# Padding the halves of an activation tile, a rotation's product in place, and two weight splits moved forward, in a two-layer decoder trunk

## The chip, the cores and the metric

The kernel runs on one core of a Trainium2 chip. Its time is the device time of one execution in microseconds (us), and the median of several executions counts. One execution was taken by the hardware profiler; the page and the answers of its trace that are quoted below come from that one. The engines are PE (TensorE, matmul), PEld (TensorE's loading of weights), DVE (VectorE), ACT (ScalarE), POOL (GpSimd) and SP (SyncE, which here only issues DMAs).

## The reference

A trunk of two layers on 256 tokens of width 2048, all in float32. Layer 0 mixes tokens by multi-scale retention with 8 heads (query and key 256 wide, value 512), layer 1 by a gated short convolution; each is followed by a SwiGLU of width 5632. Each sub-layer is normed, scaled and shifted by vectors that come from the conditioning vector c, and its output is gated and added to x.

```python
c_act = jax.nn.silu(c)
for i in range(DEPTH):
    mod = (c_act @ w_mod[i] + b_mod[i])[:, None, :]
    sh1, sc1, g1, sh2, sc2, g2 = jnp.split(mod, 6, axis=-1)
    h = (rms_norm(x, norm1_g[i]) * (1.0 + sc1) + sh1).astype(x.dtype)
...
        y = retention_mixer(h, cos, sin, ret_w_in[j], ret_w_out[j])
...
    x = (x + g1 * y).astype(x.dtype)
    h = (rms_norm(x, norm2_g[i]) * (1.0 + sc2) + sh2).astype(x.dtype)
    x = (x + g2 * swiglu(h, ffn_w_in[i], ffn_w_out[i])).astype(x.dtype)
return rms_norm(x, final_g).astype(x.dtype)
```

In the retention, q and k are rotated: `[t1 * cos - t2 * sin, t2 * cos + t1 * sin]` for the two halves t1, t2 of a head.

## The kernel before

**Layout.** The width lies on the partitions: x is 16 tiles of 128 by 256 tokens. The weights were put on the host into one array, `w_all`, in the order of their use, in chunks of 128 by 2048 floats.

**Precision.** A float32 factor is used as two parts of the type float32r: hi, the value rounded, and lo, what is left. A product is hi x hi + hi x lo + lo x hi. So an activation tile holds two halves of 256 columns, its hi in front of its lo. For h these halves lie in one tile, `h_all` (16 tiles x 2 halves x 258 columns; the 2 columns behind each half take the shift, so that a norm can be applied after the product). The other activation tiles, `mid` (input of the second matmul of the SwiGLU and of the convolution) and `rm` (the same for the retention), hold 2 x 256 columns end to end.

**Weights.** `fetch` (L293) loads a chunk into one of 3 buffers `raw`. `prepare` makes one half of a chunk, called a part, ready: ACT casts it to `hi` (L312), DVE subtracts to get `lo` (L315). There are 4 buffers of `hi` and of `lo`. `take` hands the weights to PE in 128 columns at a time and calls `prepare` when a part is used up, so that up to three parts are in hand.

**Matmuls.** `product` (L357, L360) does a block of 128 output rows with two matmuls: the weights' hi past both halves of the activation at once, 512 columns, and their lo past the first half, 256 columns. These two are called a pair. `packed` (L397 to L399) uses three matmuls of 256 columns, and puts two blocks into one PSUM bank. For the values, `by_token` (L372 to L374) takes slices of h as the stationary tile and streams 512 columns of weights. `normed` (L516 to L518) does the first columns of a sub-layer with 258 columns, before the norm is known.

**The start.** The first stretch of about 190 us interleaves the norm and modulation of layer 0 (its rows of h are made one at a time: sums of `w_mod` with c by DVE, L642; scale and shift by ACT, L667 and L670; lo by DVE, L671) with four spans of the retention's input product, `RET_SPANS`. A span runs over some of the 16 rows for some heads, holds 4 to 8 banks of sums, and at its end the sums are put aside by `held`: copied by ACT (L629), or added by DVE to what lies there (L626). Heads 0 to 3 are finished later; head 4 is done whole in the last span, and its sums stay in PSUM (`ahead`). In the start the order of ACT and DVE is the order in which the code is written (`manual_schedule`); PE's order is so throughout. Elsewhere a scheduler orders ACT, DVE, POOL and SP. The loads of a stage are all issued by SP, which waits for the buffer of one load before it issues the next.

**The rotation.** `rope` (L806 to L814) multiplies the sums of q or k by cos into `qa` (512 columns), by sin into `qb` (two operations of 256 columns that exchange the halves), then subtracts and adds halves, and splits the result into hi and lo. Its input is a tile `qs` where earlier sums were added (heads 0 to 3), PSUM otherwise.

Of the kernel before, what the change touches and what calls it, by code (L numbers as in the profile page):

```python
# [11 lines left out]
F32R = mybir.dt.float32r  # L12
I32 = mybir.dt.int32
AF = mybir.ActivationFunctionType
ALU = mybir.AluOpType
PSUM = bass.MemoryType.PSUM

P = 128
D = 2048
S = 256  # L20
KT = D // P
# [27 lines left out]
STEPS = (8, 8, 20)  # L49
RAW_BUFS = 3  # L50
PART_BUFS = 4

Q0, K0, V0, G0 = 0, HEADS * DK, 2 * HEADS * DK, 2 * HEADS * DK + HEADS * DV
SH1, SC1, GT1, SH2, SC2, GT2 = range(6)
# [71 lines left out]
RET_SPANS, RET_HEADS = ret_in_groups()  # L126
# [61 lines left out]
def trunk(ctx: ExitStack, tc: tile.TileContext, x_in, c_in, pos_in, w_mod, cols_in, tab_in, w_all, out):  # L188
    nc = tc.nc
    const = ctx.enter_context(tc.tile_pool(name="const", bufs=1))  # L190
    work = ctx.enter_context(tc.tile_pool(name="work", bufs=2))
    wpool = ctx.enter_context(tc.tile_pool(name="wpool", bufs=PART_BUFS))
    ps = ctx.enter_context(tc.tile_pool(name="ps", bufs=8, space=PSUM))
# [3 lines left out]
    def name(s):  # L197
        serial[0] += 1
        return f"{s}_{serial[0]}"

    def tmp(tag, shape=(P, S), dtype=F32, pool=work, bufs=None):
        return pool.tile(list(shape), dtype, tag=tag, name=name(tag), bufs=bufs)
# [78 lines left out]
    def needed(layer, which, last=KT - 1):  # L281
        while any(m[:2] == (layer, which) and m[2] <= last for m in todo):
            modulation(*todo.pop())
# [7 lines left out]
    def fetch():  # L291
        raw = wpool.tile([P, CHUNK], F32, tag="raw", name=name("raw"), bufs=RAW_BUFS)
        nc.sync.dma_start(raw, w_all[n_fetched[0]])  # L293
        n_fetched[0] += 1
        fetched.append(raw)

    def prepare(between=None):
        n = prepared[0]
        if n == n_halves:
            return  # L300
        prepared[0] += 1
        i = n * HALF % CHUNK
        if i == 0:
            if not fetched:
                fetch()
            raws[:] = [fetched.pop(0)]
            while first <= units[0] < early and len(fetched) < RAW_BUFS - 1 and n_fetched[0] < w_all.shape[0]:
                fetch()
        raw = raws[0][:, i : i + HALF]
        hi = wpool.tile([P, HALF], F32R, tag="hi", name=name("hi"))  # L310
        lo = wpool.tile([P, HALF], F32R, tag="lo", name=name("lo"))
        nc.scalar.copy(hi, raw)  # L312
        if between:
            between()
        nc.vector.tensor_tensor(lo, raw, hi.bitcast(F32), op=ALU.subtract)  # L315
        ready.append((hi, lo))
# [18 lines left out]
    def bank():  # L335
        return ps.tile([P, 2, S], F32, tag="bank", name=name("bank"))
# [139 lines left out]
    def modulated(h, j, rb, layer, norm):  # L476
        shifted(h, scaled(j, rb, layer, norm), j, layer, norm)

    hpool = ctx.enter_context(tc.tile_pool(name="hpool", bufs=1))

    h_all = hpool.tile([P, KT, 2, S + 2], F32R, tag="h", name="h")
    h = [h_all[:, j, :, :S] for j in range(KT)]

    def scaled_only(layer, norm, j):
# [8 lines left out]
    def normed(accs, layer, norm, g):  # L493

        needed(layer, SH2 if norm else SH1)
        shift = mod_s[layer][norm].unsqueeze(2).to_broadcast([P, KT, 2])  # L500
        ends = [h_all[:, :, i, S:] for i in range(2)]
        nc.scalar.copy(ends[0], shift)
        nc.vector.tensor_tensor(ends[1], shift, ends[0].bitcast(F32), op=ALU.subtract)
        banks = [bank().rearrange("p a b -> p (a b)")[:, : S + 2] for _ in g.cols]
        made = [0]

        def more(n):
            while made[0] < n:
                modulated(h[made[0]], made[0], root, layer, norm)
                made[0] += 1  # L510

        for k in g.ks:
            rows = [h_all[:, k, i, :] for i in range(2)]
            for c, pt in zip(g.cols, banks):
                hi, lo = take(g, k, c)
                nc.tensor.matmul(pt, hi, rows[0], start=k == 0, stop=False)  # L516
                nc.tensor.matmul(pt, hi, rows[1], start=False, stop=False)  # L517
                nc.tensor.matmul(pt, lo, rows[0], start=False, stop=k == KT - 1)  # L518
            if k == ROOTS_AT:
                r = norm_roots(norm_sums(accs), D)  # L520
            elif k == SPREAD_AT:
                root = tmp("rb", bufs=1)
                nc.scalar.copy(root, norm_spread(r))
            elif k > SPREAD_AT:
                more(min(k, made[0] + 2))
        more(KT)
        paced(len(g.cols) * len(g.ks))

        def total(pt, dst=None):
            end = tmp("end", (P, 1), bufs=2)  # L530
            nc.scalar.copy(end, pt[:, S : S + 1])
            t = tmp("low", bufs=3)
            nc.vector.tensor_tensor(t, pt[:, :S], root, op=ALU.mult)
            dst = tmp("sum", bufs=4) if dst is None else dst
            nc.scalar.activation(dst, t, AF.Identity, bias=end)
            return dst

        return [lambda dst=None, pt=pt: total(pt, dst) for pt in banks]
# [27 lines left out]
    with ExitStack() as inner:  # L566
# [46 lines left out]
        sin = rm.tile([P, S], F32, tag="sin", name="sin")  # L613
        cos = rm.tile([P, S], F32, tag="cos", name="cos")
        ahead = {}
# [15 lines left out]
        with tc.tile_pool(name="start", bufs=1) as sp:  # L631
# [59 lines left out]
            with tc.manual_schedule(engines={mybir.EngineType.DVE, mybir.EngineType.Activation}):  # L691
# [16 lines left out]
                for i in range(0, D, 2 * S):  # L708
                    pt = bank().rearrange("p a b -> p (a b)")
# [24 lines left out]
                pt = norm_sums([acc[0][:, 0, :]])  # L734
# [23 lines left out]
                pts = packed(RET_SPANS[0], h, before=before, between=both_reduced, banks=banks)  # L758
# [20 lines left out]
            def span(g):  # L779
                n = g.n // 2  # L780
                return packed(
                    g, h, before=lambda k: more(n), between=lambda k: more(n), banks=[bank() for _ in range(n)]
                )

            with tc.manual_schedule(engines={mybir.EngineType.DVE, mybir.EngineType.Activation}):
                for i, pt in enumerate(span(RET_SPANS[1])):
                    held((2 + i // 4, i % 4), pt)
                pts = span(RET_SPANS[2])
                for i, pt in enumerate(pts):
                    if i < 4:  # L790
                        held(divmod(i, 4), pt)
                    else:
                        due.append((step[0] + 0.2 * (i - 4), lambda i=i, pt=pt: held(divmod(i, 4), pt)))
                due.sort(key=lambda d: d[0])
                for i, pt in enumerate(span(RET_SPANS[3])):
                    ahead[4, i] = pt
                while due:
                    due.pop(0)[1]()
# [2 lines left out]

        rp = inner.enter_context(tc.tile_pool(name="rpool", bufs=1))

        def rope(s, tag):
            a = tmp("qa", (P, 2, S), pool=rp, bufs=1)
            nc.vector.tensor_tensor(a, s, cos.unsqueeze(1).to_broadcast([P, 2, S]), op=ALU.mult)  # L806
            b = tmp("qb", (P, 2, S), pool=rp, bufs=1)
            nc.vector.tensor_tensor(b[:, 0, :], s[:, 1, :], sin, op=ALU.mult)
            nc.vector.tensor_tensor(b[:, 1, :], s[:, 0, :], sin, op=ALU.mult)
            nc.vector.tensor_tensor(a[:, 0, :], a[:, 0, :], b[:, 0, :], op=ALU.subtract)  # L810
            nc.vector.tensor_tensor(a[:, 1, :], a[:, 1, :], b[:, 1, :], op=ALU.add)
            dst = rp.tile([P, 2, 2, S], F32R, tag=tag, name=name(tag))
            nc.scalar.copy(dst[:, 0, :, :], a)
            nc.vector.tensor_tensor(dst[:, 1, :, :], a, dst[:, 0, :, :].bitcast(F32), op=ALU.subtract)  # L814
            return dst
# [83 lines left out]
        def pair(head, i):  # L899

            g = RET_HEADS[head][0][i]
            if not g.ks:
                return [ahead[head, n] for n in ((i,) if i < 2 else (2, 3))]
            sums = packed(g, h)
            for j, pt in enumerate(sums):
                key = (head, i + j)
                if key in tag_of:
                    free.append(tag_of.pop(key))
                if key in ahead:
                    s = tmp("qs", (P, 2, S), pool=rp, bufs=1)  # L910
                    nc.vector.tensor_tensor(s, ahead[key], pt, op=ALU.add)
                    sums[j] = s
            return sums

        def projections(head):
            q = rope(*pair(head, 0), "q")
            k = rope(*pair(head, 1), "k")
            v = values(head, RET_HEADS[head][1])
            sp = scores(head, q, k)
            sg = [gate(s) for s in pair(head, 2)]  # L920
            asides.extend(mixed(head, sp, v, sg))
            since[0] = 0
# [48 lines left out]
    for i, g in enumerate(CONV_IN):  # L971
        pending += [sums(g)] if i else normed(acc, 1, 0, g)
        while len(pending) >= 3:
# [3 lines left out]
            b, c, u = pb(tmp("bsum", pool=mpool, bufs=2)), pc(), pu()  # L977
# [73 lines left out]
```

## Time and profile before

| what | value |
|---|---|
| median of 3 runs | 2645.53 us (2645.07 to 2647.69) |
| the profiled execution | 2641.89 us |
| its span, first to last instruction | 2640.1 us |
| granted TensorE clock | 0.998 of full speed |
| loaded from HBM | 682.99 MB, 259 GB/s over the span |

How to read the rows below. In rows of groups: the line of the code, engine, operation, what is written and what it is made from, its shape, how often; then the busy time in us, the mean length of one in ns; then the engine's idle time just before, and what ended it. Busy time is the time in which at least one instruction of the group ran. PE's matmuls overlap: the next one begins before the last one's results are all written. In rows of a time line: start in us, length in us, engine, line, operation, tiles, how many were merged; in brackets the idle time before the first and what ended it. In rows of waits: who waited <- for whom, total us, how often, the longest.

### The profile page before, as it was taken

The page shows a single profiled execution, that of the slowest core. Times are in us where ns is not written, and L with a number is a line of the kernel's source. Part 1 is how long each engine was busy: PE and PEld are TensorE (multiplying, and loading weights), DVE is VectorE, ACT ScalarE, POOL GpSimd, SP SyncE. Part 2 cuts the span into 40 slices and gives each one's busy share as a digit, 9 for nine tenths or more (in the row PEclk, how much of TensorE's full clock was granted, in tenths as well). Part 3 has the DMA queues.
Part 4 walks back from the last instruction along what each step waited for, and adds up shares of the span by engine and source line. Part 5 has one row for each costly group of instructions (what it writes and reads, how often), then busy time and mean ns, then how long its engine had stood idle before and what let it go on. Part 6 is the DMA issues. An engine that isn't in the chain of part 4 may idle for free.

```text
span 2640.1 us, 38225 instructions
## 1 busy us (share of the span) xinstructions
PE 2608.1 (99%) x15220; PEld 2291.2 (87%) x15220; DVE 1990.3 (75%) x2543; ACT 1244.8 (47%) x1770; POOL 146.6 (6%) x230
## 2 busy tenths in 40 slices
PE   7999999999999999999999999999999999999998
PEld 5888889888889888888888898888988888888887
DVE  7998878777698877777777888888886765555554
ACT  5644443444455444344444454444554443444443
POOL 0000001010000011110100001100000000000000
PEclk9999999999999999999999999999999999999999
DMA  9976668776686877777777768777677655555553
GB/s 397 391 273 256 258 242 317 258 271 259 251 300 243 314 283 272 273 283 283 287 270 282 268 224 321 280 281 262 253 277 263 248 219 191 190 191 187 183 190 127
DMA packets 96950, 687.58 MB, mean 260 GB/s; under 512 B 10753, under 2 KB 12545, under 8 KB 13825
## 3 DMA queue, kind: packets, MB, share of 16 engines
q1 hardware_dynamic: 96770, 685.13, 70.0%
q8 instruction: 119, 1.95, 0.3%
q14 instruction: 61, 0.50, 0.1%
HBM read 682.99 MB, written 2.10 MB: 259 GB/s over the span
## 4 chain that ended last, share of the span: by engine, by line
PE 76%; issue 19%; DVE 2%; DMA 1%; ACT 1%; POOL 0%; DVEq 0%; POOLq 0%; ACTq 0%
PE bank L357 35%; PE bank L360 18%; PE bank L372 4%; PE bank L373 4%; PE bank L374 4%; PE bank L399 2%; PE bank L398 2%; PE bank L397 2%; PE bank L517 1%; PE bank L516 1%; PE bank L518 1%; DVE raw L642 1%; DMA raw<-w_all 1%; PE bank L869 1%; DVE lo L315 1%
## 5 line engine op out<-in xcount | busy, mean ns | idle before, releaser
L315 DVE TENSOR_TENSOR lo<-raw,hi 128x1024 fp32r<-128x1024 f32 x912 | 1111.5, 1222 | 551.6 <-ACT hi L312 549.3
L312 ACT CAST hi<-raw 128x1024 fp32r<-128x1024 f32 x912 | 953.2, 1050 | 1088.9 <-PE bank L357 649.0
L357 PE MATMUL bank<-h,hi 128*128 128x512 f32 x3296 | 1155.2, 395 | 0.0
L360 PE MATMUL bank<-h,lo 128*128 128x256 f32 x3296 | 924.4, 280 | 0.0
L357 PEld LDWEIGHTS bank<-h,hi 128*128 128x128 f32 x3296 | 622.6, 189 | 145.3
L360 PEld LDWEIGHTS bank<-h,lo 128*128 128x128 f32 x3296 | 622.0, 189 | 0.0
L357 PE MATMUL bank<-mid,hi 128*128 128x512 f32 x1604 | 556.3, 393 | 0.0
L360 PE MATMUL bank<-mid,lo 128*128 128x256 f32 x1604 | 444.9, 277 | 0.6 <-DVE lo L315 0.6
L246 DVE SCALAR_TENSOR_TENSOR raw<-raw,cb 128x2048 f32<-128x2048 f32 x160 | 365.4, 2284 | 11.7 <-DMA raw<-w_mod 11.3
L357 PEld LDWEIGHTS bank<-mid,hi 128*128 128x128 f32 x1604 | 300.7, 187 | 69.4
L360 PEld LDWEIGHTS bank<-mid,lo 128*128 128x128 f32 x1604 | 301.3, 188 | 0.9 <-DVE lo L315 0.9
L372 PE MATMUL bank<-hi,h 128*128 128x512 f32 x512 | 202.7, 396 | 0.0
L373 PE MATMUL bank<-lo,h 128*128 128x512 f32 x512 | 201.9, 394 | 0.0
L374 PE MATMUL bank<-hi,h 128*128 128x512 f32 x512 | 201.9, 394 | 0.0
L357 PE MATMUL bank<-rm,hi 128*128 128x512 f32 x496 | 174.2, 396 | 0.0
L399 PE MATMUL bank<-h,lo 128*128 128x256 f32 x512 | 145.6, 284 | 9.1 <-DVE lo L315 9.1
L397 PE MATMUL bank<-h,hi 128*128 128x256 f32 x512 | 144.9, 283 | 2.5 <-ACT h L670 2.5
L398 PE MATMUL bank<-h,hi 128*128 128x256 f32 x512 | 144.8, 283 | 0.5 <-DVE h L671 0.5
L360 PE MATMUL bank<-rm,lo 128*128 128x256 f32 x496 | 138.5, 279 | 0.0
L374 PEld LDWEIGHTS bank<-hi,h 128*128 128x128 f32 x512 | 96.3, 188 | 22.7
L372 PEld LDWEIGHTS bank<-hi,h 128*128 128x128 f32 x512 | 96.6, 189 | 19.6
L373 PEld LDWEIGHTS bank<-lo,h 128*128 128x128 f32 x512 | 96.4, 188 | 19.6
(152 smaller groups left out, 2239.3 us busy)
## 6 DMA issues: line engine op xcount, KB each, us to landing
raw<-w_all SPq DMA_DIRECT2D x456, 1024.0 KB, 4.8
raw<-w_mod SPq DMA_DIRECT2D x192, 1024.0 KB, 5.0
x<-x_in SPq DMA_DIRECT2D x4, 512.0 KB, 5.7
out<-out SPq DMA_DIRECT2D x5, 256.0 KB, 3.4
decay<-tab_in SPq DMA_DIRECT2D x8, 128.0 KB, 2.2
out<-out SPq DMA_DIRECT2D x3, 128.0 KB, 2.5
out<-out SPq DMA_DIRECT2D x1, 384.0 KB, 2.7
cols<-cols_in SPq DMA_DIRECT2D x1, 160.0 KB, 8.8
```

The lines of the kernel that those rows point to most:

```text
L246: nc.vector.scalar_tensor_tensor(raw, raw, 1.0, cb, op0=ALU.mult, op1=ALU.mult, accum_out=total)
L312: nc.scalar.copy(hi, raw)
L315: nc.vector.tensor_tensor(lo, raw, hi.bitcast(F32), op=ALU.subtract)
L357: nc.tensor.matmul(pt, hi, h, start=fresh and k == g.ks[0], stop=False, skip_group_check=True)
L360: nc.tensor.matmul(pt[:, 1, :], lo, h[:, 0, :], start=False, stop=last and k == g.ks[-1], skip_group_check=True)
L372: nc.tensor.matmul(o, ht[:, 0, :], hi, start=first, stop=False)
L373: nc.tensor.matmul(o, ht[:, 0, :], lo, start=False, stop=False)
L374: nc.tensor.matmul(o, ht[:, 1, :], hi, start=False, stop=last)
L397: nc.tensor.matmul(pt, hi, h[:, 0, :], start=first, stop=False, skip_group_check=True)
L398: nc.tensor.matmul(pt, hi, h[:, 1, :], start=False, stop=False, skip_group_check=True)
L399: nc.tensor.matmul(pt, lo, h[:, 0, :], start=False, stop=last, skip_group_check=True)
L516: nc.tensor.matmul(pt, hi, rows[0], start=k == 0, stop=False)
```

## The change

Three edits. The halves of h lie 272 columns apart (1088 bytes) where they lay 258 apart (1032 bytes). The rotation multiplies both halves by sin in one operation of 512 columns, which writes over its input where that input is the kernel's own (`ours`: sums that were held or put into `ahead`), and into a tile `qs` otherwise; subtraction and addition read the exchanged halves; the tile `qb` is gone. At the ends of the second and third span `prepare` is called once in front of `held`, so the cast and subtraction of one more part stand in front of the copies or additions on ACT and DVE, and with them the load that `prepare` issues on SP.

```diff
+PAD = 16
...
-    h_all = hpool.tile([P, KT, 2, S + 2], F32R, tag="h", name="h")
+    h_all = hpool.tile([P, KT, 2, S + PAD], F32R, tag="h", name="h")
...
-        ends = [h_all[:, :, i, S:] for i in range(2)]
+        ends = [h_all[:, :, i, S : S + 2] for i in range(2)]
...
-            rows = [h_all[:, k, i, :] for i in range(2)]
+            rows = [h_all[:, k, i, : S + 2] for i in range(2)]
...
-                for i, pt in enumerate(span(RET_SPANS[1])):
+                pts = span(RET_SPANS[1])
+                prepare()
+                for i, pt in enumerate(pts):
                     held((2 + i // 4, i % 4), pt)
                 pts = span(RET_SPANS[2])
+                prepare()
                 for i, pt in enumerate(pts):
...
-        def rope(s, tag):
+        def rope(s, tag, ours):
...
-            b = tmp("qb", (P, 2, S), pool=rp, bufs=1)
-            nc.vector.tensor_tensor(b[:, 0, :], s[:, 1, :], sin, op=ALU.mult)
-            nc.vector.tensor_tensor(b[:, 1, :], s[:, 0, :], sin, op=ALU.mult)
-            nc.vector.tensor_tensor(a[:, 0, :], a[:, 0, :], b[:, 0, :], op=ALU.subtract)
-            nc.vector.tensor_tensor(a[:, 1, :], a[:, 1, :], b[:, 1, :], op=ALU.add)
+            b = s if ours else tmp("qs", (P, 2, S), pool=rp, bufs=1)
+            nc.vector.tensor_tensor(b, s, sin.unsqueeze(1).to_broadcast([P, 2, S]), op=ALU.mult)
+            nc.vector.tensor_tensor(a[:, 0, :], a[:, 0, :], b[:, 1, :], op=ALU.subtract)
+            nc.vector.tensor_tensor(a[:, 1, :], a[:, 1, :], b[:, 0, :], op=ALU.add)
...
-            q = rope(*pair(head, 0), "q")
-            k = rope(*pair(head, 1), "k")
+            q = rope(*pair(head, 0), "q", (head, 0) in ahead)
+            k = rope(*pair(head, 1), "k", (head, 1) in ahead)
```

## Prediction

> **What bounds the kernel now.** I read the page's table of engines first, then its costliest groups, then the waits of PE, and then groups and time lines of single stretches.
>
> ```profile
> span 2640.1 us, 38225 instructions
> PE 2608.1 (99%) x15220; PEld 2291.2 (87%) x15220; DVE 1990.3 (75%) x2543; ACT 1244.8 (47%) x1770; POOL 146.6 (6%) x230
> ```
>
> The span lies in an execution of 2641.89 us, 1.8 us more. The runs' median, 2645.53, is 3.6 us above that execution, and I add these 3.6 us to every sum. PE is busy 99%; what isn't busy stands in the waits of PE:
>
> ```profile
> PE bank L399 <- DVE lo L315: 9.1, 6, 2.3
> PE bank L433 <- DVE sq L733: 3.2, 1, 3.2
> PE bank L397 <- ACT h L670: 2.5, 1, 2.5
> PE bank L360 <- DVE lo L315: 0.6, 1, 0.6
> ...
> 260.00:400.00 140.00, 140.00 (x753) 119.86 (x752) 112.88 (x153) 63.56 (x88) 8.60 (x13) 1.00 0.67 247
> 400.00:600.00 200.00, 200.00 (x1159) 175.45 (x1158) 159.93 (x196) 86.43 (x111) 21.99 (x37) 1.00 0.78 285
> ```
>
> (The last two are rows of the windows: stretch, its length, busy time of PE, PEld, DVE, ACT, POOL with counts, granted clock, DMA share and GB/s.) From about 155 us to 2620 us PE stands still once, for 0.6 us. Over nine tenths of the span an edit can pay only by changing how fast PE streams. That rate is read from the groups of the page:
>
> ```profile
> L357 PE MATMUL bank<-h,hi 128*128 128x512 f32 x3296 | 1155.2, 395 | 0.0
> L357 PE MATMUL bank<-mid,hi 128*128 128x512 f32 x1604 | 556.3, 393 | 0.0
> L357 PE MATMUL bank<-rm,hi 128*128 128x512 f32 x496 | 174.2, 396 | 0.0
> ```
>
> A pair is one L357 matmul (both halves of an activation tile stream past the weights' high part) and one L360 matmul (the first half past their low part). One L357 matmul lasts 395 ns and the next begins before it has ended, so this line is busy without a gap, and busy time by count is the time from pair to pair: 1155.2 / 3296 = **350.5 ns** on h, 556.3 / 1604 = **346.8 ns** on mid, 174.2 / 496 = 351.2 ns on rm. Same shapes, same weights, another address. The 512-column stream of h lies in two runs 1032 bytes apart (258 floats); mid and rm hold their halves end to end. In the built program every one of these tiles, and the weights too, begins 32 bytes past a multiple of 64.
>
> **Part 1, the padding.** It adds and removes no instruction. It moves the halves of h from 1032 to 1088 bytes apart, so that all 32 halves begin 32 bytes past a multiple of 64, as mid's do; before, they began at every multiple of 8. That address decides something is seen inside h, in PE's time line:
>
> ```profile
> 1200.31 0.39 PE L357 MATMUL bank<-h,hi 128*128 128x512 f32 x1
> 1200.65 0.39 PE L357 MATMUL bank<-h,hi 128*128 128x512 f32 x1
> ...
> 1202.04 0.40 PE L357 MATMUL bank<-h,hi 128*128 128x512 f32 x1
> 1202.40 0.40 PE L357 MATMUL bank<-h,hi 128*128 128x512 f32 x1
> ```
>
> One pair takes 0.34 us, another 0.36, with nothing waited for. If the placing of mid gives the rate of mid, each of the 3296 pairs on h gets 350.5 - 346.8 = 3.7 ns shorter: 3296 x 3.7 = **12.2 us less**. No row shows this placing with a 64-byte hole between the halves, so both ends stay: 341 ns (the 0.34 us pair) for 31 us less, and the slowest lasting rate on tiles placed like mid, which is this:
>
> ```profile
> L357 PE MATMUL bank<-rm,hi 128*128 128x512 f32 x151 | 52.4, 393 | 0.0
> ...
> L357 PE MATMUL bank<-rm,hi 128*128 128x512 f32 x185 | 65.4, 399 | 0.0
> ```
>
> These are two stretches of the same line on rm, 377 to 429 us and 713 to 778 us. The first runs at 52.4 / 151 = 347.0 ns, the second at 65.4 / 185 = 353.5. The high end is therefore (353.5 - 350.5) x 3296 = 9.9 us more. I take mid's value, since all long stretches on mid agree with it and the fast stretch of rm too.
>
> The other readers of h: the packed triples (L397 to L399) and the products in which a slice of h is the stationary tile (L372 to L374).
>
> ```profile
> L397 PE MATMUL bank<-h,hi 128*128 128x256 f32 x512 | 144.9, 283 | 2.5 <-ACT h L670 2.5
> L397 PE MATMUL bank<-mid,hi 128*128 128x256 f32 x60 | 17.0, 283 | 0.0
> L373 PE MATMUL bank<-lo,h 128*128 128x512 f32 x512 | 201.9, 394 | 0.0
> L869 PE MATMUL bank<-v,sp 128*128 128x512 f32 x72 | 19.1, 392 | 0.0
> ```
>
> Triples take the same on h and on mid: 0. With h stationary, 394 against 392 where both tiles are placed like mid: at most 2 ns x 1536 = 3 us less; I take 0 and keep the 3. The padding makes h 1792 bytes longer and moves rm, mid and all behind them by that much; they stay 32 past a multiple of 64, so I cost it at 0, but see the second rival.
>
> **Part 2, the rotation.** Two products of 256 columns become one of 512, sixteen times.
>
> ```profile
> L808 DVE TENSOR_TENSOR qb<-bank,sin 128x256 f32<-128x256 f32 x8 | 3.3, 414 | 0.0
> L809 DVE TENSOR_TENSOR qb<-bank,sin 128x256 f32<-128x256 f32 x8 | 3.3, 412 | 0.0
> L806 DVE TENSOR_TENSOR qa<-bank,cos 128x512 f32<-128x512 f32 x8 | 5.5, 691 | 5.8 <-PE bank L399 3.9 <-ACT cos L606 1.8
> ```
>
> DVE saves 414 + 412 - 691 = 135 ns each, 2.2 us in all. They run between 190 and 650 us, where the windows above show PE full, so it is worth 0; without that cover it would be 2.2 us. Where the sums lie in PSUM and are ours (head 4) the product is written back there; no row shows such a write, and twice a 691 ns operation gained or lost, hidden by the same full PE, bounds it. That bank is held two operations of 416 ns longer; PE waits for no bank there.
>
> **Part 3, two splits moved forward.** At two span ends, the next part's hi (ACT, L312) and lo (DVE, L315) go in front of the eight sums' copies or additions.
>
> ```profile
> 92.29 1.05 ACT L312 CAST hi<-raw 128x1024 fp32r<-128x1024 f32 x1 [1.78 <-PE bank L374]
> 93.24 5.25 ACT L629 COPY rm<-bank 128x512 f32<-128x512 f32 x8
> 99.50 0.59 ACT L670 ACTIVATE h<-two,s,a 128x256 fp32r<-128x256 f32 x1
> 99.99 2.93 ACT L312 CAST hi<-raw 128x1024 fp32r<-128x1024 f32 x3
> ...
> 87.76 5.58 SPq L293 DMA_DIRECT2D raw<-w_all  x2
> 93.40 2.16 SPq L238 DMA_DIRECT2D raw<-w_mod  x2
> 97.50 0.33 SPq L293 DMA_DIRECT2D raw<-w_all  x1
> ...
> raw<-w_all SPq DMA_DIRECT2D x1, 1024.0 KB, 8.7
> ...
> 97.71 0.28 PE L397 MATMUL bank<-h,hi 128*128 128x256 f32 x1
> ```
>
> First place. The part now cast at 99.99 comes from the load issued at 87.76, which lands 8.7 us later, at 96.5. Moved in front of the copies, this cast ends at 97.5 and all eight copies stand behind it: the first ends 0.6 later, at 98.1, while PE's next span asks for its bank at 97.71: 0.4 us of a new wait. The copies, no longer paced by PE, end near 101.5 instead of 98.4; the row of h behind them (L670) slips by 3 us. The lo itself gains: DVE does it in idle time.
>
> ```profile
> 100.12 0.43 DVE L671 TENSOR_TENSOR h<-u,h 128x256 fp32r<-128x256 f32 x1 [2.64 <-ACT h L670]
> 101.06 1.23 DVE L315 TENSOR_TENSOR lo<-raw,hi 128x1024 fp32r<-128x1024 f32 x1 [0.51 <-ACT hi L312]
> 102.20 2.29 DVE L642 SCALAR_TENSOR_TENSOR raw<-raw,cb 128x2048 f32<-128x2048 f32 x1
> ```
>
> But L671 now ends at 103.6, so L642 starts 1.4 us later than 102.20, and the lo's behind it, for one of which PE already waits at 109.6, come 1.4 late. On SP the weight load of 97.50 passes the two w_mod loads of 93.40, which now start at 97.8; their sums (L642) stand a whole row of h later, near 112 us: no cost. Second place:
>
> ```profile
> 142.46 2.47 DVE L626 TENSOR_TENSOR rm<-rm,bank 128x512 f32<-128x512 f32 x4
> 147.66 1.22 DVE L315 TENSOR_TENSOR lo<-raw,hi 128x1024 fp32r<-128x1024 f32 x1
> 152.81 1.22 DVE L315 TENSOR_TENSOR lo<-raw,hi 128x1024 fp32r<-128x1024 f32 x1
> ...
> 154.08 0.39 PE L399 MATMUL bank<-h,lo 128*128 128x256 f32 x1 [1.92 <-DVE lo L315]
> ```
>
> The lo of 147.66 moves in front of the additions of 142.46, whose first bank comes 1.2 us later; PE wants it at 143.4 and stops for 1.1. But DVE works from 142 to 154 without a pause and in sum the same, so the lo of 152.81 keeps its time, and PE's wait of 1.92 there shrinks by what it lost. A delay from the first place may be swallowed there too. Part 3: 0 to 1.4 us more; I take 0.7, the middle, as neither end is nearer.
>
> **Sum:** 2641.9 - 12.2 + 0.7 = 2630.4 for the profiled execution, plus 3.6: **2634 us**.
>
> **Rivals.** (1) Placing does nothing lasting: rm, placed like mid, runs at 351.2 on the whole, no better than h; mid may be fast for another reason. Also, the halves begin 32 bytes past a multiple of 64, not on one, so that the change does not do what it says if the boundary itself counts. Then 2645.5 + 0.7 = 2646. Against it: all long stretches on mid, and h's own spread of pairs. The Trainium skill speaks for this rival: "TensorE: Matmul & The Clock Gate", Back-to-back issue gap, gives a lone matmul N / 2.4 + 2.5 ns, and Step-by-step says that loading the next weights takes no read bandwidth from the running matmul; neither knows an address. By it, as an estimate, a pair takes 325 ns everywhere; the trace doesn't agree, with 346.8, 347.0, 350.5 and 353.5 for one form.
>
> (2) Slower: PE's two streams, weights and activations, fall into the slow step of 353.5 ns that rm shows at 713 to 778 us. In h before, the offset changes from tile to tile, which I take to break such a step up; a constant placing would let it last. Its place is the five long stretches on h from 820 us on. At 353.5 everywhere: 9.9 + 0.7, thus 2656. It decides from the point where more than (350.5 - 346.8) / (353.5 - 346.8) = 55% of the pairs on h are in it. If it also catches mid, moved by 1792 bytes, 1604 x 6.7 = 10.7 more. For it: 185 of rm's 496 pairs stand in that one stretch, at an unchanged placing. Against: no long stretch on mid is.
>
> (3) More: h gets better than mid, between 341 and 346 ns, since its offset against the weights steps by 128 bytes from tile to tile: 15 to 31 us less, 2615 to 2630.
>
> **How the numbers follow.** Forecast 0.50, rival 1 0.18, rival 2 0.22, rival 3 0.10. A measurement here tells 0.2%, 5.3 us, from no change. Faster: 0.50 + 0.10 = 0.60; same: 0.18; slower: 0.22. The range reaches from the upper part of rival 3, 2626, to all of h in the slow step, 2656; outside lie most of rival 3 and the case that mid is caught too.
>
> **What would show it.** Right: L357 on h at 346 to 348 ns by busy time over count, mid unchanged, PE's other times unchanged. Wrong: h at 350 (rival 1), at 353 with L357 lasting 399 ns on average (rival 2), or mid or rm off their present rates. Part 3 is right if PE waits for a bank near 97.7 and 143.4 us, and the wait at 154 us is shorter. The forecast falls with the assumption that a rate belongs to a placing.

## The result, and the profile after

The changed kernel took 2650.37 us (median of 19 runs, 2648.91 to 2656.58), the kernel before 2644.84 us on the same chip (19 runs): a ratio of 1.0022, 95% interval 1.0015 to 1.003. It is 5.5 us slower; the forecast was 2634. The profiled execution took 2649.91 us. Line numbers are one higher than before, from the spans of the start on by some more. The page's head, and its rows of groups for the pairs:

```profile
span 2648.1 us, 38217 instructions
PE 2615.5 (99%) x15220; PEld 2297.6 (87%) x15220; DVE 1989.9 (75%) x2527; ACT 1244.6 (47%) x1770; POOL 153.3 (6%) x230
...
L358 PE MATMUL bank<-h,hi 128*128 128x512 f32 x3296 | 1153.8, 393 | 0.0
...
L358 PE MATMUL bank<-mid,hi 128*128 128x512 f32 x1604 | 567.0, 399 | 0.0
...
L358 PE MATMUL bank<-rm,hi 128*128 128x512 f32 x496 | 174.3, 397 | 0.0
```

Busy time over count again gives the time of a pair. On h it fell from 350.5 to 350.1 ns: 1.4 us in all, where 12.2 were expected. On mid, whose code and shapes are untouched, it rose from 346.8 to 353.5 ns: 10.7 us. On rm it stayed, 351.2 before and 351.4 after. PE's busy time rose by 7.4 us, the span by 8.0: PE still never waits there, it streams more slowly. (8.0 us between the two profiled executions and 5.5 between the medians: the profiled execution of before lies 3.0 under its median.)

The same line in one stretch of mid (1040 to 1150 us) and one of h (1160 to 1400 us), of before and then of after, with the windows of after around the stretches (columns as in the rows of windows above):

```profile
L357 PE MATMUL bank<-mid,hi 128*128 128x512 f32 x319 | 110.6, 393 | 0.0
...
L357 PE MATMUL bank<-h,hi 128*128 128x512 f32 x686 | 240.4, 395 | 0.0
```

```profile
L358 PE MATMUL bank<-mid,hi 128*128 128x512 f32 x313 | 110.6, 399 | 0.0
...
L358 PE MATMUL bank<-h,hi 128*128 128x512 f32 x687 | 240.5, 393 | 0.0
```

```profile
820.00:1032.00 212.00, 212.00 (x1213) 186.14 (x1212) 166.89 (x204) 105.89 (x167) 16.54 (x28) 1.00 0.79 291
1033.00:1156.00 123.00, 123.00 (x698) 106.73 (x697) 90.26 (x99) 46.39 (x46) 13.95 (x20) 1.00 0.73 270
```

In the same 110.6 us PE began 319 pairs of mid before and 313 after: 346.7 and 353.4 ns. (A window cuts its first and last pair, so such a quotient is good to about 1 ns.) The granted clock is 1.00 in both stretches, so it isn't the clock, and PE has no gap. From the starts of the single pairs, every long stretch on h and on mid has one mean, held from beginning to end: before 350.4 on h and 346.7 on mid, after 350.0 on h and 353.3 on mid. Such a lasting mean is called a step below. Mid is in the fast step before and in the slow step after, the step of 353.5 that rm showed at 713 to 778 us in the kernel before.

The other parts. The waits of PE between 95 and 160 us, of before and of after; then ACT and DVE of after at the two places:

```profile
PE bank L399 <- DVE lo L315: 2.2, 2, 1.9
```

```profile
PE bank L400 <- DVE lo L316: 1.6, 2, 0.8
PE bank L398 <- DVE rm L627: 0.8, 1, 0.8
```

```profile
96.74 1.05 ACT L313 CAST hi<-raw 128x1024 fp32r<-128x1024 f32 x1 [3.14 <-DMA raw<-w_all]
97.70 3.99 ACT L630 COPY rm<-bank 128x512 f32<-128x512 f32 x8
```

```profile
142.76 2.36 DVE L316 TENSOR_TENSOR lo<-raw,hi 128x1024 fp32r<-128x1024 f32 x2 [0.51 <-ACT hi L313]
145.04 2.48 DVE L627 TENSOR_TENSOR rm<-rm,bank 128x512 f32<-128x512 f32 x4
```

The moved split stands in front of the copies and of the additions. PE's time line of after, at the first place, then at the later waits:

```profile
97.58 0.39 PE L374 MATMUL bank<-lo,h 128*128 128x512 f32 x1
97.81 0.39 PE L375 MATMUL bank<-hi,h 128*128 128x512 f32 x1
98.32 0.39 PE L398 MATMUL bank<-h,hi 128*128 128x256 f32 x1
```

```profile
111.09 0.38 PE L400 MATMUL bank<-h,lo 128*128 128x256 f32 x1 [0.83 <-DVE lo L316]
...
145.87 0.36 PE L398 MATMUL bank<-h,hi 128*128 128x256 f32 x1 [0.84 <-DVE rm L627]
...
155.53 0.39 PE L400 MATMUL bank<-h,lo 128*128 128x256 f32 x1 [0.74 <-DVE lo L316]
```

Matmuls of this length follow each other every 0.23 us; at 98.32 the gap is 0.51, so PE lost 0.28 on its bank. At 145.87 it waits 0.84 us for the additions, and the wait of 1.92 us that stood at 154 is down to 0.74. The listed waits of this stretch come to 2.4 us after and 2.2 before.

### The profile page after: what moved, and what is told of

It is laid out like the page before. It is cut to its first block, busy times and chain, and to the rows that moved or that the text cites. A ratio compares the mean times of both kernels' runs of the same rounds, so it can differ in the third digit from the quotient of the medians.

```text
span 2648.1 us, 38217 instructions
## 1 busy us (share of the span) xinstructions
PE 2615.5 (99%) x15220; PEld 2297.6 (87%) x15220; DVE 1989.9 (75%) x2527; ACT 1244.6 (47%) x1770; POOL 153.3 (6%) x230
## 4 chain that ended last, share of the span: by engine, by line
PE 74%; issue 20%; DVE 3%; DMA 2%; ACT 1%; SPq 0%; POOL 0%; DVEq 0%; ACTq 0%; POOLq 0%
PE bank L358 35%; PE bank L361 18%; PE bank L374 4%; PE bank L373 4%; PE bank L375 4%; PE bank L398 2%; PE bank L400 2%; PE bank L399 2%; DMA raw<-w_all 2%; DVE raw L643 1%; PE bank L517 1%; PE bank L519 1%; PE bank L518 1%; DVE lo L316 1%; PE bank L873 1%
## 5 line engine op out<-in xcount | busy, mean ns | idle before, releaser
L358 PE MATMUL bank<-mid,hi 128*128 128x512 f32 x1604 | 567.0, 399 | 0.0
L361 PE MATMUL bank<-mid,lo 128*128 128x256 f32 x1604 | 450.5, 281 | 0.0
```

Source lines behind the costliest of these rows:

```text
L358: nc.tensor.matmul(pt, hi, h, start=fresh and k == g.ks[0], stop=False, skip_group_check=True)
L361: nc.tensor.matmul(pt[:, 1, :], lo, h[:, 0, :], start=False, stop=last and k == g.ks[-1], skip_group_check=True)
```

## The experiments

Ratios are to the kernel before on the same chip. One execution of each run was profiled, and the steps are read from that one. Two theories stood after the result. **A, place:** mid was moved by 1792 bytes, and the new place makes it slow. **B, history:** a long stretch on mid keeps whichever step it enters with, and the padded h hands PE over in the slow one. The rival to both is that another part of the change does it.

**e1_mid_back** and **e2_mid_moved** separate A from B: after with mid put back to the same remainder modulo 2048 bytes, and before with mid moved by the change's 1792 bytes.

```diff
 # e1, in after
+    mpool.tile([P, 64], F32, tag="gap", name="gap")
 # e2, in before
+    mpool.tile([P, 448], F32, tag="gap", name="gap")
```

> The changed kernel with a hole of 256 bytes in front of mid, so that mid lies 1056 bytes past a multiple of 2048 as it did in the kernel before (800 in the changed one, where the weights hi and lo lie too); h stays padded, rm stays moved. Theory A (place: a pair on mid is slow because mid lies at the weights' offset): mid back at 347 ns a pair instead of 353, 1604 x 6.2 = 9.9 us less than the changed kernel's 2650.4, so 2640.5, which is 4 us under the kernel before; h stays at 350. Theory B (history: PE enters mid from a padded h in another step and nothing breaks it up): mid stays at 353, 2650.4.

> The kernel before with a hole of 1792 bytes in front of mid, so that mid alone moves to where the changed kernel has it; h, the rotation and the splits are those of before. Theory A (place): mid goes from 347 to 353 ns a pair, 2644.8 + 9.9 = 2654.7. Theory B (history): h before leaves PE in the same step, mid stays at 347, 2644.8.

e1: 2650.24 us, 1.0026 (1.0015 to 1.0037). e2: 2644.79 us, 1.0001 (0.9992 to 1.001). The stretch 1040 to 1150 us of e1, then of e2:

```profile
L358 PE MATMUL bank<-mid,hi 128*128 128x512 f32 x312 | 110.3, 399 | 0.0
```

```profile
L357 PE MATMUL bank<-mid,hi 128*128 128x512 f32 x318 | 110.3, 394 | 0.0
```

353.5 and 346.9 ns: the place of mid doesn't set the step. A falls. (All five stretches on mid begin so in both runs; one of them, the convolution's, changes over midway, in e1 from slow to fast and in e2 from fast to slow. More on this with e3.)

**e3_no_padding** and **e4_no_splits** take parts of the change away.

```diff
 # e3, in after
-PAD = 16
+PAD = 2
 # e4, in after
-                prepare()
...
-                prepare()
```

> The changed kernel without the padding (PAD = 2): the rotation and the two splits alone. Both theories: h at 350.5 and mid at 347 as before; what is left is the start, 0 to 1.4 us by the prediction, so 2644.8 to 2646.2. A rival to both, that the loss comes from the splits or the rotation: 2650.

> The changed kernel without the two splits moved forward: padding and rotation alone. Both theories: mid slow at 353, h at 350, 9.9 - 1.3 us above before, and 0 to 1.4 us under the changed kernel: 2649 to 2650.4. If the splits cost more than was read from the start, it falls below 2649.

e3: 2645.3 us, 1.0008 (0.9999 to 1.0016), mid back at 346.7 in four of its five stretches. e4: 2651.01 us, 1.0028 (1.0017 to 1.0039), mid at 353.3 throughout. So it is the padding that makes the loss; of the splits and the rotation nothing can be told from no change. The fifth stretch of e3 (the convolution's) shows how a step can end. Its wait in PE's time line, then pairs from 1800 to 1826 us and from 1830 to 1875 us:

```profile
1828.03 0.39 PE L361 MATMUL bank<-mid,lo 128*128 128x256 f32 x1 [1.00 <-DVE lo L316]
```

```profile
L358 PE MATMUL bank<-mid,hi 128*128 128x512 f32 x76 | 26.4, 394 | 0.0
```

```profile
L358 PE MATMUL bank<-mid,hi 128*128 128x512 f32 x129 | 45.6, 399 | 0.0
```

346.7 ns by the starts of the pairs in front of the wait (26.4 / 76 is 347.4, cut at the edges), 353.3 behind it, on the same tiles. One stall of PE can be enough to change the step. It needn't be: at the same place the kernel before waits 0.60 us and e14 (below) 0.88 us and both keep their step, while 0.78 us turn e1 from slow to fast. In e2 there is no listed wait at all, only one pair of 379 ns in front of the change.

**e5_kick_after** and **e7_kick_before** disturb PE on purpose: one extra short matmul, of 32, 64, 96, 128 and 192 columns, in front of the five stretches on mid. Its result is overwritten.

```diff
+                if kick:
+                    nc.tensor.matmul(
+                        pt[:, 0, :kick], hi, h[:, 0, :kick], start=True, stop=False, skip_group_check=True
+                    )
+                    kick = 0
```

> The changed kernel with one short extra matmul in front of the first pair of each of the five long stretches on mid (32, 64, 96, 128 and 192 columns in this order; its sum is overwritten). No address and no order moves; only the moment in PE's step at which the stretch begins does. History (a stretch keeps the step in which it starts): at least one of the five leaves 353.3 ns a pair for 346.7; each one that does takes 240 to 352 pairs x 6.6 ns = 1.6 to 2.3 us off 2650.4, all five 10. Place, or anything else that is fixed by addresses: all five stay at 353.3, and the time at 2650.4 plus five times about 0.1 us.

> The kernel before with the same five short matmuls in front of the stretches on mid. History: at least one of the long stretches leaves 346.7 ns a pair for 353.3 (1.6 to 2.3 us more each, up to 10 on 2644). Anything fixed by addresses: all stay at 346.7, 2644 to 2645.

e5: 2648.68 us, 1.0015 (1.0006 to 1.0024). e7: 2648.81 us, 1.0019 (1.001 to 1.0028). The first and the last stretch on mid (1040 to 1150 and 2515 to 2615 us) of e5, then of e7:

```profile
L365 PE MATMUL bank<-mid,hi 128*128 128x512 f32 x312 | 110.3, 399 | 0.0
...
L365 PE MATMUL bank<-mid,hi 128*128 128x512 f32 x289 | 100.2, 391 | 0.0
```

```profile
L364 PE MATMUL bank<-mid,hi 128*128 128x512 f32 x319 | 110.6, 393 | 0.0
...
L364 PE MATMUL bank<-mid,hi 128*128 128x512 f32 x284 | 100.4, 399 | 0.0
```

In the changed kernel the last stretch went from 353.5 to 346.7 ns (100.2 / 289), in the kernel before the last two went from 346.7 to 353.5; the other seven began in the step that they have without a kick. No address differs and no work but one matmul of at most 192 columns: B holds, both ways, in that a stretch keeps the step with which it begins and the step isn't fixed by addresses. Which kick flips a stretch didn't follow from its length alone (128 flipped in e7 and not in e5).

**e6_end_to_end** and **e8_pad8** ask why h itself stayed at 350.0. In e6 the halves of h lie end to end as those of mid do, the shift's columns in front of the first and behind the second, still 2176 bytes from tile to tile; in e8 the padding is 8 columns, 1056 bytes between the halves.

```diff
 # e6, in after
-    h_all = hpool.tile([P, KT, 2, S + PAD], F32R, tag="h", name="h")
+    h_all = hpool.tile([P, KT, PAD + 2 * S + PAD], F32R, tag="h", name="h")
...
-            rows = [h_all[:, k, i, : S + 2] for i in range(2)]
+            rows = [h_all[:, k, PAD - 2 : PAD + S], h_all[:, k, PAD + S : PAD + 2 * S + 2]]
 # e8, in after
-PAD = 16
+PAD = 8
```

> The changed kernel with the halves of h end to end, as mid and rm have them: the two extra columns lie in front of the first half and behind the second, 2176 bytes from tile to tile as in the changed kernel, the halves 32 past a multiple of 64. The first columns of a sub-layer write the second half's products two columns further, and one tiny addition more joins the two shifts (18 times). History: h now meets the same steps as mid and rm, 346.7 or 353.3 ns a pair and no longer 350.0: either 3296 x 3.3 = 11 us less or 11 more than the changed kernel's 2650.4, and mid goes with it, fast or slow (0 or 10 less): 2629, 2639, 2651 or 2661. If the hole of 64 bytes has no part in the 350.0: h stays at 350.0, 2650.

> The changed kernel with PAD = 8: the halves lie 1056 bytes apart, at multiples of 32 and by turns on a multiple of 64 and 32 past one; mid moves by 1024 less. If a boundary of 64 bytes decides, h falls below 350.0 ns, where every other half lies on one. History: h settles on some mean of its own between 341 and 357, and mid takes 346.7 or 353.3 from the step that h leaves, whatever mid's own place: 2640 or 2650 at h = 350.

e6: 2652.09 us, 1.0029 (1.0018 to 1.0041). e8: 2645.26 us, 1.0005 (0.9996 to 1.0014). The page's rows of e6, then of e8:

```profile
L358 PE MATMUL bank<-h,hi 128*128 128x512 f32 x3296 | 1153.8, 395 | 0.0
...
L358 PE MATMUL bank<-mid,hi 128*128 128x512 f32 x1604 | 565.9, 398 | 0.0
```

```profile
L358 PE MATMUL bank<-h,hi 128*128 128x512 f32 x3296 | 1153.8, 393 | 0.0
...
L358 PE MATMUL bank<-mid,hi 128*128 128x512 f32 x1604 | 557.4, 392 | 0.0
```

h is at 350.1 in both. At 2176 bytes from tile to tile the hole between the halves thus changes nothing; e8 changed the hole, the places within 64 bytes and the distance of the tiles (2112) at once. And e8 has mid in the fast step again, in four of its five stretches and at the start of the fifth: between 1.0022 and 1.0005 lie 4.5 us, which hang on the padding of h by way of mid. What is left for h is the **pitch**, the distance from tile to tile, and with it how the tile's address moves against that of the weights, from pair to pair. Theory P: the pitch sets h's mean. Theory Q: something else does, such as the work beside it.

**e9_pitch_2048, e10_pitches, e11_pitches** try pitches: 2048, mid's own, in e9 (no padding, halves end to end; the kernel leaves out the columns of the shift); in e10 and e11, laid out as e6, another for each later h.

```diff
 # e9, in after
-    h_all = hpool.tile([P, KT, 2, S + PAD], F32R, tag="h", name="h")
+    h_all = hpool.tile([P, KT, 2, S], F32R, tag="h", name="h")
 # e10, in e6: floats from tile to tile, by layer and sub-layer
+PITCH = {(0, 0): 544, (0, 1): 516, (1, 0): 520, (1, 1): 536}
 # e11
+PITCH = {(0, 0): 544, (0, 1): 524, (1, 0): 528, (1, 1): 540}
```

> The kernel after, with the tiles of h 2048 bytes apart, halves end to end, as those of mid lie. The two columns behind each half are left out, so the products of the first columns of a sub-layer lack the norm's shift, which this kernel does not compute there; its matmuls have 256 in place of 258 columns at these places. Theory P (the step from tile to tile sets the mean of h: 2176 bytes in the kernel after, 2064 before, 2048 on mid): h comes off 350.0 ns a pair, to 346.7 or 353.3 as mid has, so 3296 x 3.3 = 11 us less or more on h. Theory Q (h is at 350.0 for another reason, such as what DVE and ACT do beside it): h stays at 350.0, and the time stays at 2645 to 2650 according to which step mid takes.

> As the run in which the halves of h lie end to end with 2176 bytes from tile to tile, but with another pitch for each later h: 2064 bytes in the first SwiGLU, 2080 in the convolution, 2144 in the second SwiGLU (2176 stays in the retention). Theory P: the mean of h differs between these pitches by steps of 3.3 ns (346.7, 350.0, 353.3), constant within a stretch. Theory Q: 350.0 at all of them (350.4 at most at 2064). mid takes 346.7 or 353.3 behind each, and only that moves the time, between 2640 and 2651.

> The same with 2096 bytes in the first SwiGLU, 2112 in the convolution, 2160 in the second SwiGLU. Theory P: some of these leave 350.0 by 3.3 ns; 2112 and 2160 bytes, odd and even multiples of 16 and 64, are the likeliest to differ from each other. Theory Q: 350.0 at all three, and the time is set by the step that mid takes, 2640 to 2651.

e9: 2657.09 us, 1.0051 (1.0036 to 1.0066). e10: 2648.8 us, 1.0017 (1.0007 to 1.0026). e11: 2651.88 us, 1.0031 (1.0018 to 1.0044). One stretch on h of e9 (1165 to 1395 us); three of e10 with 2064, 2080 and 2144 bytes (830 to 1030, 1570 to 1790, 1935 to 2130 us); the same three of e11 with 2096, 2112 and 2160:

```profile
L357 PE MATMUL bank<-h,hi 128*128 128x512 f32 x652 | 230.4, 399 | 0.0
```

```profile
L359 PE MATMUL bank<-h,hi 128*128 128x512 f32 x569 | 200.4, 396 | 0.0
...
L359 PE MATMUL bank<-h,hi 128*128 128x512 f32 x628 | 220.4, 395 | 0.0
...
L359 PE MATMUL bank<-h,hi 128*128 128x512 f32 x562 | 195.3, 392 | 0.0
```

```profile
L359 PE MATMUL bank<-h,hi 128*128 128x512 f32 x570 | 200.3, 395 | 0.0
...
L359 PE MATMUL bank<-h,hi 128*128 128x512 f32 x632 | 220.7, 393 | 0.0
...
L359 PE MATMUL bank<-h,hi 128*128 128x512 f32 x556 | 195.3, 395 | 0.0
```

By the starts of the pairs: 2048 bytes 353.3 ns, 2064 352.1, 2080 350.8, 2096 351.2, 2112 349.2, 2144 347.5, 2160 351.2; and 2176 350.0. Two stretches at one pitch agree to 0.1. Q falls. That the means stand apart only in steps of 3.3 ns, as P expected, was wrong too: at the pitches of e10 and e11 the single pairs go through many lengths, from 339 to 362 ns, and the mean lies between. Nor does the pitch alone set the mean: with a hole between the halves h runs at 350.4 at 2064 bytes (before) and at 350.0 at 2112 (e8), where it takes 352.1 and 349.2 end to end.

Mid brought a second miss. It was expected at 346.7 or 353.3, but the first two of its stretches run at 348.9 in both e10 and e11, from beginning to end; here e10, 1045 to 1150 us:

```profile
L359 PE MATMUL bank<-mid,hi 128*128 128x512 f32 x302 | 105.4, 393 | 0.0
```

So mid, at 2048 bytes, has at least three lasting means.

**e12_pad12** and **e13_2144** take the best of these pitches, 2144 bytes, for every h: e12 in the change's own layout (halves 1072 bytes apart), e13 in that of e6. **e14_2144_kick** adds a matmul of 192 columns ahead of each stretch on mid to e13. **e15_2048_kick** puts e5's five kicks in front of the stretches on h in e9, and like e9 leaves out the shift's columns.

```diff
 # e12, in after
-PAD = 16
+PAD = 12
 # e13, in e10
+PITCH = {key: 536 for key in ((0, 0), (0, 1), (1, 0), (1, 1))}
```

> The kernel after with PAD = 12 in place of 16: the tiles of h 2144 bytes apart, the halves 1072. Theory P (the step from tile to tile sets the mean of h): h near 347.5 ns a pair, as it ran at 2144 bytes with halves end to end, 3296 x 2.5 = 8 us less on h than in the kernel after. mid then takes 346.7 (time 2635) or 353.3 (time 2645). Theory Q (only the place of the halves counts, and 350.0 belongs to any padding): h at 350.0, time 2644 to 2651.

> The layout with the halves of h end to end, at 2144 bytes from tile to tile in every sub-layer. Theory P: h at 347.5 ns a pair in all its stretches, mid at 353.3 as behind the stretch that ran so before; time 2645 to 2647. If another state decides and not the pitch: h between 350 and 352.

> The same with one extra matmul of 192 columns in front of each of the five stretches on mid. If the step on mid is what PE happens to be left in: mid leaves 353.3 for 346.7 in some or all stretches, up to 1604 x 6.6 = 10.6 us less than without, time 2635 to 2641. If the step on mid follows from the pitch of h ahead of it whatever is run between: 353.3 throughout and 2646.

> The kernel with the tiles of h 2048 bytes apart (the norm's shift left out of the first columns of a sub-layer) with one extra matmul of 32, 64, 96, 128 and 192 columns in front of its five stretches on h. If a tile pitch like mid's has two lasting steps, as mid has, some of the stretches on h leave 353.3 for 346.7 ns, and mid behind them takes the same step; one stretch of 704 pairs is worth 4.7 us. If 353.3 belongs to the addresses: all five stay at 353.3.

e12: 2645.83 us, 1.0007 (0.9997 to 1.0016). e13: 2644.79 us, 1.0000 (0.9991 to 1.001). e14: 2645.7 us, 1.0003 (0.9994 to 1.0012). e15: 2652.59 us in one run. Two stretches on h of e12 (830 to 1025, 1165 to 1395 us); the page's rows of e13:

```profile
L358 PE MATMUL bank<-h,hi 128*128 128x512 f32 x560 | 195.3, 393 | 0.0
...
L358 PE MATMUL bank<-h,hi 128*128 128x512 f32 x658 | 230.3, 394 | 0.0
```

```profile
L359 PE MATMUL bank<-h,hi 128*128 128x512 f32 x3296 | 1145.7, 392 | 0.0
...
L359 PE MATMUL bank<-mid,hi 128*128 128x512 f32 x1604 | 567.0, 396 | 0.0
```

e13 has h at 347.6 in all five stretches, 9.5 us less than before, and gives the whole of it back on mid, which stands at 353.5. In e12 the same pitch with a hole between the halves gives 348.7 in three stretches and 350.0 in two, with mid slow behind the three and fast behind the two: the pitch is not all, and 2144 bytes too have two means. In e14, 192 columns, which had flipped a stretch in e5 and in e7, flipped none: its second case came, 353.3 throughout, in which the step on mid follows from the h ahead of it. e15 settled mid's own pitch. Its stretches on h at 1165 to 1395 and 2275 to 2500 us, and on mid at 1410 to 1510 us:

```profile
L362 PE MATMUL bank<-h,hi 128*128 128x512 f32 x664 | 230.2, 391 | 0.0
```

```profile
L362 PE MATMUL bank<-h,hi 128*128 128x512 f32 x638 | 225.5, 399 | 0.0
```

```profile
L362 PE MATMUL bank<-mid,hi 128*128 128x512 f32 x289 | 100.2, 391 | 0.0
```

h at 2048 bytes ran at 353.4 in four stretches and, after the kick of 64 columns, at 346.7 (230.2 / 664) in the other, the second, and the mid behind that one took 346.7 from it, where it stands at 353.3 in e9. Two lasting steps at one set of addresses, and here they are handed on. Of the twenty kicks of e5, e7, e14 and e15 four flipped a stretch.

**e16_mid_too** gives the tiles of mid, in e13, another pitch than 2048 as well.

```diff
+    def spaced(pool, tag, what):
+        t = pool.tile([P, 536], F32R, tag=tag, name=name(what))
+        return t[:, : 2 * S].rearrange("p (a b) -> p a b", a=2)
```

> The layout with h at 2144 bytes from tile to tile, and mid too: each tile of mid gets 96 unused bytes behind it. Theory P (the step between tiles decides, whatever engine state came before): mid at 347.5 ns a pair in every stretch, as h is, in place of 353.3: 1604 x 5.8 = 9.3 us less than with h alone, 2635 to 2636, a ratio of 0.997 to the kernel before. If mid's slow step is handed on whatever its addresses: 353.3 again and 2645.

2639.57 us (11 runs), before 2642.86 on the same chip: 0.9987 (0.9978 to 0.9996). Its page:

```profile
L359 PE MATMUL bank<-h,hi 128*128 128x512 f32 x3296 | 1145.8, 392 | 0.0
...
L359 PE MATMUL bank<-mid,hi 128*128 128x512 f32 x1604 | 560.4, 394 | 0.0
```

Mid came off the slow step to 349.4 ns, the same in its four longer stretches, where 347.5 was expected. The fifth, the convolution's, has both. PE waits 0.48 us for a lo before 1824.64 us; pairs from 1800 to 1822 us and from 1826 to 1875 us:

```profile
L359 PE MATMUL bank<-mid,hi 128*128 128x512 f32 x64 | 22.4, 394 | 0.0
```

```profile
L359 PE MATMUL bank<-mid,hi 128*128 128x512 f32 x142 | 49.4, 392 | 0.0
```

22.4 / 64 is 350.0, cut at the edges, and 49.4 / 142 is 347.9; by the starts of the pairs mid takes 347.5 behind the wait. So the pitch of 2144 bytes keeps mid off 353.3 here, but it doesn't leave one step only. This version is faster than before by 3.3 us, and than the changed kernel by some 9 if the runs of before beside each are set equal (0.9987 against 1.0022).

## Why the prediction was wrong, point by point

**What bounds the kernel:** right. In the long stretches PE streams with hardly a gap before and after; of the 8.0 us between the two spans 7.4 are busy time of PE, at unchanged counts.

**Part 1:** the step that failed is "If the placing of mid gives the rate of mid", with the last sentence of the prediction, "a rate belongs to a placing". e9 lays h out as mid lies, and h takes 353.3; e15 has this one placing with 346.7 and 353.4, and e5 and e7 do the same to mid. Mid's 346.7 in the kernel before was one of several steps that its placing allows. So h got 350.0, the mean of its own layout, and 3296 x 0.4 = 1.3 us in place of 12.2. The second term that failed is "rm, mid and all behind them … I cost it at 0": mid cost 10.7 us. The amount stands in the second rival (1604 x 6.7), but the reason given there, the move by 1792 bytes, is refuted by e1 and e2. What showed in its place: the step on mid hangs on the layout of the h that runs ahead of it (e3, e8), and the padded h leaves mid in the slow one.

The warning was in the rows that the prediction quotes: rm at 347.0 and at 353.5 ns, one form and one placing. The prediction used this pair of rows as the ends of a range for h, and didn't ask what it says of mid: that 346.8 is one of two states and can be lost.

**Rival 1** was right on h, in that the boundary of 64 bytes doesn't give the rate: end to end at 2048, 2112 and 2176 bytes every half of h begins at the same place within 64 bytes, and h takes 353.3, 349.2 and 350.0 (e9, e11, e6). By its total, 2646, it was 4 us low for want of mid. **Rival 2** was right that a slow step exists and can hold long stretches, wrong about where: all of mid, none of h. The reason against it, that no long stretch on mid is in that step, counted five stretches in one step as five witnesses for the placing, though all of them stood behind the same h. **Rival 3** is out at this layout (350.0 against 341 to 346).

**Part 2:** the products run as costed (691 ns), and the write to PSUM, which no row had shown, takes 690 ns where the others take 681 to 685:

```profile
L813 DVE TENSOR_TENSOR qs<-qs,sin 128x512 f32<-128x512 f32 x8 | 5.5, 685 | 0.1
...
L813 DVE TENSOR_TENSOR qs<-bank,sin 128x512 f32<-128x512 f32 x6 | 4.1, 681 | 0.0
L813 DVE TENSOR_TENSOR bank<-bank,sin 128x512 f32<-128x512 f32 x2 | 1.4, 690 | 0.0
```

**Part 3:** right in mechanism at both places. At the first, 0.28 us of a new wait (0.4 forecast) and the lo that PE waits for 1.5 later (111.09 against 109.6, with 1.4 forecast). At the second, 0.84 us (1.1 forecast), most of it given back at the next wait. Together 0.2 us more of listed waits and the 0.28; e4 can't tell it from nothing. One trace can't either: e2, whose code in the start is that of before, reaches its first pair on h at 823.73 us, before at 820.37.

What the runs do show of the step in which mid begins: without a kick it is the same behind every stretch of h of one layout and mean. It is fast behind 350.4 (before, e2, e3) and behind e8's 350.0, slow behind the 350.0 at 2176 bytes (after, e1, e4, e6) and behind 347.5 (e13); in e12 it changes with the mean of h. So it isn't chance, but no rule was found that gives it from the addresses.

What stays open: that rule, which kick or stall changes a step, and by what mechanism PE holds it. The runs show that addresses and history both matter; that the two streams that PE reads, weights and activations, disturb each other is an argument, not a finding. The Trainium skill, in "TensorE: Matmul & The Clock Gate", Step-by-step, says that loading the next tile's weights takes no read bandwidth from the running matmul; no run here measured the two streams apart.

## What to carry to other kernels

When one form of instruction shows two rates at one placing anywhere in a trace, treat the rate of every other stretch as a state and not as a property of its layout: a layout's rate is known only once it has been seen to come back after a stall. Look at what stands ahead of a long stretch without stalls, since an edit there can cost more in the next stretch than it gains in its own. Another distance between the tiles is worth a trial, but doesn't make the rate a property of the layout: at 2144 bytes too a stream had two means (e12 on h, e16 on mid).

## What the runs showed of the hardware that was not expected

- With tiles 2048 bytes apart, a pair of 512 and 256 float32r columns takes 346.7 or 353.3 ns on average through whole stretches, 2% apart, at a granted clock of 1.00, and 348.9 in some stretches of e10 and e11. One stall of 1.0 us (e3), or one extra matmul of 64 to 192 columns (e5, e7, e15), changed 346.7 for 353.3 or back; a stall of 0.88 us (e14) and most kicks didn't.
- The mean depends on the pitch of the tiles by up to 5.8 ns: 347.5 at 2144 bytes, 353.3 at 2048 in the slow step. It depends on the hole between the halves too: 350.4 with one of 8 bytes at a pitch of 2064, 352.1 end to end.
- A constant mean hides alternating pairs: padded h goes 349, 351, 349, 351; the fast step 346, 347, 347 (e15) or 350, 343, 350, 344 (before); the slow one 349, 350, 361 (after) or 348, 357, 355 (e13).
